# A feed-forward first product by seven block products instead of eight, in two of three channel-tile pairs

## The chip, the core and the metric

The kernel runs on one core of a Trainium2 chip. The metric is the device time of one execution in microseconds (us). The engines that matter here are PE (TensorE, the matrix products), DVE (VectorE) and ACT (ScalarE), which prepare its operands, POOL (GpSimd), and SP, whose queue starts the loads from device memory.

## What is computed

One layer of a streaming encoder over 256 tokens and 2048 channels: a mixer of three branches (a gated linear recurrence, an attention with forget gates, a multi-scale pooling), an output projection, and then the part that changes here, a gated feed-forward network (FFN) with 5632 inner channels.

```python
    x = x + merged @ w_out
    h2 = rms_norm(x, g_ffn)
    gate, up = jnp.split(h2 @ w_ffn_in, 2, axis=-1)
    return x + (jax.nn.silu(gate) * up) @ w_ffn_out
```

`h2 @ w_ffn_in` is called the first product here and the product with `w_ffn_out` the second. A final norm follows.

## The kernel before

All operands are float32, and every product is taken in three parts: each number is split into a high part and a low part (`float32r`), and high times high, high times low and low times high are added up. A weight block arrives by a load of 1 MB on SP's queue (`load`, line 59, three buffers), and `split` (line 64) makes the two parts of 1024 columns at a time: ACT copies to `whi` (line 69), DVE subtracts to get `wlo` (line 70). Four pairs of `whi` and `wlo` exist (pool `hl`, line 46), so the splits can stand at most four half blocks ahead of PE.

The activations lie transposed, channels on the partitions. `mm_t` (line 79) takes for each contraction tile of 128 a product of 512 columns, `whi` against both parts of the activations, and one of 256 columns, `wlo` against the high part; this pair of instructions does three parts. `evac_t` (line 95) adds the two halves. `mm_n` (line 87) does the same as three products of 256 columns into one place, and is used for the last tile of the second product alone.

Up to the FFN the order is: the mixer, `mT` (the merged branches, as two parts), the output projection (line 571, 16 tiles), which also writes `h2` (the FFN's input times its norm gain, in the tile called `hT`). The FFN's first product (line 590) runs over 44 channel tiles; each takes two column blocks with K = 2048 (`proj_t`, one for the gate and one for the up half), 32 pairs of products in all, and its result goes to `act` in two parts. The second product (line 613) runs over 16 output tiles, each with 44 contraction tiles. A scheduler sets the order on each engine; splits and evacuations may overtake other work (`tc.high_priority`). Each engine works through its instructions in that order, and SP's queue its loads; a wait at the front holds everything behind it.

Of the kernel before, what the change touches and what calls it, by code (L numbers as in the profile page):

```python
# [7 lines left out]
F32 = mybir.dt.float32  # L8
# [30 lines left out]
def block_kernel(ctx: ExitStack, tc: tile.TileContext, xT, vec,  # L39
# [5 lines left out]
    raw_p = ctx.enter_context(tc.tile_pool(name="raw", bufs=3))  # L45
    hl_p = ctx.enter_context(tc.tile_pool(name="hl", bufs=4))
    acc_p = ctx.enter_context(tc.tile_pool(name="acc", bufs=4, space=bass.MemoryType.PSUM))
    aux_p = ctx.enter_context(tc.tile_pool(name="aux", bufs=4, space=bass.MemoryType.PSUM))
    hT_p = ctx.enter_context(tc.tile_pool(name="hT", bufs=1))
    sm = ctx.enter_context(tc.tile_pool(name="sm", bufs=2))  # L50

# [34 lines left out]
    # the same in columns 0..255 alone: a longer product, a shorter way out  # L86
# [8 lines left out]
    def evac_t(ps, dst, scale=1.0):  # L95
        """Adds the two halves of a transposed product, times scale, into dst [128, 256]."""
# [17 lines left out]
    hT = hT_p.tile([P, KD, 2 * T], F32R, name="hT")  # [hi | lo] of x * g_mix, transposed  # L114
    vecs = const.tile([P, NV], F32, name="vecs")
    x_p = ctx.enter_context(tc.tile_pool(name="x", bufs=1))
    xt = x_p.tile([P, KD, T], F32, name="xt")  # x, then the residual stream, transposed
# [4 lines left out]
    vhl = at_p.tile([P, 2, 2, DB], F32R, name="vhl", bufs=1)  # token tile, part, channel  # L122
# [5 lines left out]
    warm = aux()  # keeps the array clocked up until the first operands are there  # L128
# [3 lines left out]
    def prepare_x(k):  # L132
        """Contraction tile k of x * g_mix as two parts, and its share of the sum of squares."""
# [12 lines left out]
    def rsqrt_mean(dst, ss, n, pool, nm):  # L146
        """dst (or two factors of it) = (ss / D + eps) ** -0.5, with one Newton step behind the table's root."""
# [45 lines left out]
    for c in (0, 2):  # keep where query >= key  # L193
# [3 lines left out]
    tri = at_p.tile([P, 2, T], F32, name="tri", bufs=1)  # 1 where row s (+128) <= t  # L197
# [4 lines left out]
    # F(query) - F(key) as one product: LF holds F^T and minus the selector of a head, RF the  # L202
    # selector and F^T; F in rows 0.. (high part) and 32.. (low), or 64.. and 96..
# [12 lines left out]
    def stats():  # L216
        """The factors 1 / rms(x), along the rows and in columns."""
# [10 lines left out]
    def normalise(k):  # L228
        """Contraction tile k of h, in the place of that of x * g_mix."""
# [43 lines left out]
    # minus half of log a for a recurrence gate of one  # L273
# [29 lines left out]
    def scores(h, q, k):  # L303
        """Softmax of head h's scores, transposed: [keys 0 | queries 0, 1], [keys 1 | queries 1]."""
# [10 lines left out]
        ns = at_p.tile([P, 3 * P], F32, name="ns")  # minus the scores  # L315
        st = at_p.tile([P, 8], F32, name="st")  # minus the maxima, sums, their reciprocals
# [77 lines left out]
    def lru_in(g):  # L394
# [22 lines left out]
        # gelu(y) = y (1 + tanh(c (y + 0.044715 y^3))) / 2  # L417
# [8 lines left out]
    def lru_out(g, u, uh, ul, ga):  # L426
# [14 lines left out]
        # th = tanh(-log(a) / 2): 1 - a = 2 th / (1 + th), 1 - a^2 = (1 - a)(1 + a).  # L441
# [7 lines left out]
        V.scalar_tensor_tensor(rg, rg, 2.0, rc, ALU.mult, ALU.mult)  # 1 - a  # L449
# [18 lines left out]
    def pool_in(g):  # L468
# [6 lines left out]
        # sums over 2, 4, 8, 16 tokens, each from the one before; column c holds token c - PADW  # L475
# [6 lines left out]
        # the mean, less the token itself: the first tokens count what there is  # L482
# [29 lines left out]
    def gate(n):  # L512
        """Sigmoid of gate block n = 3 m + branch."""
# [21 lines left out]
    mx_p.release()  # L535
    mT_p = tc.alloc_tile_pool(name="mT", bufs=1)
# [23 lines left out]
    h2 = hT_p.tile([P, KD, 2 * T], F32R, name="hT")  # [hi | lo] of x2 * g_ffn, transposed  # L560
# [8 lines left out]

    s2acc = const.tile([P, T], F32, name="sacc")  # L570
    for m in range(KD):
# [3 lines left out]
        g_ = vecs[:, GF + m:GF + m + 1]  # L575
        with tc.high_priority(offset=AHEAD):
            V.tensor_add(xt[:, m, :], xt[:, m, :], o)
            S.activation(h2[:, m, :T], xt[:, m, :], AF.Copy, scale=g_)
            V.scalar_tensor_tensor(h2[:, m, T:], xt[:, m, :], g_, h2[:, m, :T].bitcast(F32),  # L579
                                   ALU.mult, ALU.subtract)  # L580
        squares(m, s2acc)
    mT_p.release()
    sg_p.release()
    yAC_p.release()
    yB_p.release()

# [1 line left out]
    ac_p = tc.alloc_tile_pool(name="act", bufs=1)  # L588
    act = ac_p.tile([P, NF, 2 * T], F32R, name="act")
    for f in range(NF):  # L590
        pg = proj_t(wffi[2 * f], lambda k: h2[:, k, :])
        pu = proj_t(wffi[2 * f + 1], lambda k: h2[:, k, :])
        if f == 0:
            ps = aux()
            PE.matmul(ps[:, :T], lhsT=ones, rhs=s2acc, start=True, stop=True)
            R2 = const.tile([P, T], F32, name="R2")
            rsqrt_mean(R2, [ps[:, :T]], T, sm, ("t0", "t1"))
        gt = sm.tile([P, T], F32, name="t0")
        up = sm.tile([P, T], F32, name="t1")
        evac_t(pg, gt)  # L600
        V.tensor_mul(gt, gt, R2)
        S.activation(gt, gt, AF.Silu)
        evac_t(pu, up)
        G.tensor_mul(up, up, R2)  # L604
        V.tensor_mul(gt, gt, up)
        S.copy(act[:, f, :T], gt)
        V.tensor_sub(act[:, f, T:], gt, act[:, f, :T].bitcast(F32))

# [4 lines left out]
    for m in range(KD):  # L613
        ps = acc()
        for a in range(0, NF, 16):
            n = min(16, NF - a)
            r = load(wffo[m, :, a * P:(a + n) * P], n * P)
            for c in range(0, n, 8):
                nk = min(8, n - c)
                hi, lo = split(r, c * P, nk * P)  # L620
                k0 = a + c
                if m == last and k0 == 32:  # the sums over all blocks but this
                    pss = [aux()[:, :1] for _ in range(2)]
# [3 lines left out]
                (mm_n if m == last else mm_t)(ps, hi, lo, lambda k, k0=k0: act[:, k0 + k, :], nk,  # L627
                                              k0 == 0, k0 + nk == NF)
        g_ = vecs[:, GL + m:GL + m + 1]
        if m < last:  # L630
            o = sm.tile([P, T], F32, name="t0")
            evac_t(ps, o)
# [93 lines left out]
```

## Time and profile before

| | us |
|---|---|
| median of three runs | 1574.26 (1574.19 to 1574.32) |
| span of the profiled execution | 1572.5 |
| FFN's first and second product, first matmul to the last tile of the second product | 725.0 |
| PE busy in the span | 1549.3 |
| DVE busy in the span | 994.3 |
| ACT busy in the span | 821.3 |

The span runs from the first to the last instruction of the profiled execution; it is 1.8 us less than the median of the timed runs. Busy time of PE counts the pipelined tail of each matmul, so the distance between the starts of two matmuls, not the length of one, says what a matmul costs. The same holds in a small way on DVE and ACT, whose instructions overlap by about 0.09 us.

### The profile page before, as it was taken

The page shows a single profiled execution, that of the slowest core. Times are in us where ns is not written, and L with a number is a line of the kernel's source. Part 1 is how long each engine was busy: PE and PEld are TensorE (multiplying, and loading weights), DVE is VectorE, ACT ScalarE, POOL GpSimd, SP SyncE. Part 2 cuts the span into 40 slices and gives each one's busy share as a digit, 9 for nine tenths or more (in the row PEclk, how much of TensorE's full clock was granted, in tenths as well). Part 3 has the DMA queues.
Part 4 walks back from the last instruction along what each step waited for, and adds up shares of the span by engine and source line. Part 5 has one row for each costly group of instructions (what it writes and reads, how often), then busy time and mean ns, then how long its engine had stood idle before and what let it go on. Part 6 is the DMA issues. An engine that isn't in the chain of part 4 may idle for free.

```text
span 1572.5 us, 22842 instructions
## 1 busy us (share of the span) xinstructions
PE 1549.3 (99%) x8948; PEld 1362.1 (87%) x8948; DVE 994.3 (63%) x1356; ACT 821.3 (52%) x1264; POOL 154.8 (10%) x210
## 2 busy tenths in 40 slices
PE   8999999999999999999999999999999999999997
PEld 8888888888888888888888888888888888888886
DVE  9776677787565656667776555555555555445453
ACT  6565566666444444445555444444444444444442
POOL 7400011102000000000110000000000000010100
PEclk9999999999999999999999999999999999999998
DMA  7444455545555455555555555555555555555552
GB/s 245 170 155 159 140 184 185 212 164 200 185 190 197 167 202 184 201 174 201 188 188 183 189 189 189 188 188 188 188 188 187 188 188 178 188 196 178 192 187 88
DMA packets 46764, 288.92 MB, mean 184 GB/s; under 512 B 5184, under 2 KB 8000, under 8 KB 15936
## 3 DMA queue, kind: packets, MB, share of 16 engines
q1 hardware_dynamic: 46080, 286.54, 52.5%
q8 instruction: 70, 1.15, 0.3%
q10 hardware_dynamic: 576, 0.92, 0.2%
q14 instruction: 38, 0.31, 0.1%
HBM read 285.34 MB, written 2.10 MB: 183 GB/s over the span
## 4 chain that ended last, share of the span: by engine, by line
PE 93%; DVE 2%; POOL 2%; issue 2%; ACT 1%; DMA 0%; SPq 0%; DVEq 0%; POOLq 0%; ACTq 0%
PE acc L82 59%; PE acc L83 30%; POOL xn L232 1%; POOL part L144 1%; DVE wlo L70 1%; ACT whi L69 0%; POOL lev L479 0%; PE acc L91 0%; PE acc L93 0%; PE acc L92 0%; DVE xt L657 0%; PE aux L338 0%; DVE lma L179 0%; PE acc L264 0%; DMA raw<-in_wvf 0%
## 5 line engine op out<-in xcount | busy, mean ns | idle before, releaser
L82 PE MATMUL acc<-hT,whi 128*128 128x512 f32 x2800 | 983.6, 395 | 0.4 <-DVE hT L579 0.4
L70 DVE TENSOR_TENSOR wlo<-raw,whi 128x1024 fp32r<-128x1024 f32 (+2 forms) x554 | 671.3, 1213 | 476.5 <-ACT whi L69 475.5
L69 ACT CAST whi<-raw 128x1024 fp32r<-128x1024 f32 (+2 forms) x554 | 567.9, 1026 | 614.2 <-PE acc L82 425.1
L83 PE MATMUL acc<-hT,wlo 128*128 128x256 f32 x2800 | 785.6, 281 | 0.0
L82 PEld LDWEIGHTS acc<-hT,whi 128*128 128x128 f32 x2800 | 526.3, 188 | 122.2 <-DVE hT L579 0.7
L83 PEld LDWEIGHTS acc<-hT,wlo 128*128 128x128 f32 x2800 | 527.2, 188 | 0.2
L82 PE MATMUL acc<-act,whi 128*128 128x512 f32 x660 | 231.1, 395 | 0.0
L83 PE MATMUL acc<-act,wlo 128*128 128x256 f32 x660 | 185.1, 280 | 0.0
L82 PEld LDWEIGHTS acc<-act,whi 128*128 128x128 f32 x660 | 124.1, 188 | 29.1
L83 PEld LDWEIGHTS acc<-act,wlo 128*128 128x128 f32 x660 | 124.3, 188 | 0.0
L100 ACT COPY evt<-acc 128x256 f32<-128x256 f32 x247 | 90.0, 365 | 0.0
L82 PE MATMUL acc<-mT,whi 128*128 128x512 f32 x256 | 89.8, 395 | 0.0
L604 POOL TENSOR_TENSOR t<-t,R 128x256 f32<-128x256 f32 x44 | 32.4, 737 | 459.3 <-DVE t L101 435.0
L83 PE MATMUL acc<-mT,wlo 128*128 128x256 f32 x256 | 71.6, 280 | 0.0
L101 DVE TENSOR_TENSOR t<-acc,evt 128x256 f32<-128x256 f32 x167 | 69.7, 417 | 1.0 <-ACT evt L100 0.9
L568 POOL TENSOR_TENSOR sacc<-sacc,t 128x256 f32<-128x256 f32 x29 | 34.6, 1195 | 293.0 <-ACT t L567 293.0
L82 PEld LDWEIGHTS acc<-mT,whi 128*128 128x128 f32 x256 | 48.1, 188 | 11.4 <-DVE mT L554 0.3
L83 PEld LDWEIGHTS acc<-mT,wlo 128*128 128x128 f32 x256 | 48.2, 188 | 0.0
L551 POOL TENSOR_TENSOR t<-t,t 128x256 f32<-128x256 f32 x16 | 11.8, 740 | 352.3 <-DVE t L549 352.3
L82 PE MATMUL acc<-yB,whi 128*128 128x512 f32 x128 | 45.5, 395 | 0.0
L82 PE MATMUL acc<-yC,whi 128*128 128x512 f32 x128 | 45.5, 395 | 0.0
L82 PE MATMUL acc<-yA,whi 128*128 128x512 f32 x128 | 45.5, 395 | 0.0
(246 smaller groups left out, 1209.9 us busy)
## 6 DMA issues: line engine op xcount, KB each, us to landing
raw<-in_wffi SPq DMA_DIRECT2D x88, 1024.0 KB, 4.8
raw<-in_wgate SPq DMA_DIRECT2D x48, 1024.0 KB, 4.8
raw<-in_wffo SPq DMA_DIRECT2D x32, 1024.0 KB, 4.9
raw<-in_wqk SPq DMA_DIRECT2D x16, 1024.0 KB, 4.8
raw<-in_wxy SPq DMA_DIRECT2D x16, 1024.0 KB, 4.9
raw<-in_wbr SPq DMA_DIRECT2D x16, 1024.0 KB, 5.0
raw<-in_wout SPq DMA_DIRECT2D x16, 1024.0 KB, 4.8
raw<-in_wffo SPq DMA_DIRECT2D x16, 768.0 KB, 4.3
```

The source lines that it names most:

```text
L69: S.copy(hi[:, :n], r[:, a:a + n])
L70: V.tensor_sub(lo[:, :n], r[:, a:a + n], hi[:, :n].bitcast(F32))
L82: PE.matmul(ps, lhsT=hi[:, w], rhs=rhs(k), start=first and k == 0, stop=False)
L83: PE.matmul(ps[:, :T], lhsT=lo[:, w], rhs=rhs(k)[:, :T], start=False, stop=last and k == nk - 1)
L100: S.copy(tmp, ps[:, T:])
L101: V.tensor_add(dst, ps[:, :T], tmp)
L144: G.tensor_add(part, part, sq)
L232: G.tensor_mul(xn, xt[:, k, :], Rrow)
L551: (G if b == 1 else V).tensor_add(tot, tot, o)
L568: G.tensor_add(sacc, sacc, sq)
L604: G.tensor_mul(up, up, R2)
```

## The change

The FFN's first product works on groups of two channel tiles: 22 groups, in four chunks of 6, 6, 6 and 4, and after each chunk the second product is taken over that chunk's channels and added to the residual stream `xt`. Operands change sides: the activations (`hs`, 128 tokens at a time) are the stationary operand and the weights the moving one, and results come out with tokens on the partitions.

A group is a 2 x 2 block product: tokens (two halves) and K (two halves) against K and the gate and up columns (256 each). `group_plain` takes the eight block products. `group_strassen` takes seven (Winograd's form of Strassen's scheme), for which the weights are needed as sums of blocks and the activations as well; the activations' four sums are made once, in the output projection (`forms`). `PATTERN` makes groups 0, 1, 3, 4, ... of the seven kind (15) and 2, 5, ... of the eight kind (7). Each block product is 24 matmuls of 256 columns. Of the four sums of weight blocks in a seven-product group, `y` and the first `x` are made by DVE (`ADDS[0]`, `ADDS[1]`), and two more are added onto `x` by DMAs that POOL issues (`accum_op`), between the splits of `x`.

The results are transposed back on PE (`turn`, four transposes a group) into `act`, which now holds one chunk. The second product uses `mm_n` everywhere. For the FFN the raw buffers become six of 8 KB (`raw6`), which are allocated on the side where `mT` and the three old raw buffers lay.

```diff
+PATTERN = (1, 1, 0)
+ADDS = ("v", "v", "dma", "dma")
+CHUNKS = (12, 12, 12, 8)
...
+    mT_p = tc.alloc_tile_pool(name="mT", bufs=1, side="right")
...
+    hs = hs_p.tile([P, KB, 8, 2, P], F32R, name="hs")
...
+    def forms(k, first, src):
+        n = src.shape[1]
+        S.copy(hs[:, k, first:first + n, 0, :], src)
+        V.tensor_sub(hs[:, k, first:first + n, 1, :], src, hs[:, k, first:first + n, 0, :].bitcast(F32))
...
+            hm = hg[:, k, :] if m < KB else hg_p.tile([P, T], F32, name="hm", bufs=2)
+            S.activation(hm, xt[:, m, :], AF.Copy, scale=vecs[:, GF + m:GF + m + 1])
+            hm = hm.rearrange("p (a b) -> p a b", a=2)
+            forms(k, m // KB * 2, hm)
+            if m >= KB:
+                a11, a21, a12, a22 = hg[:, k, :P], hg[:, k, P:], hm[:, 0, :], hm[:, 1, :]
+                c = hg_p.tile([P, 4, P], F32, name="hc", bufs=2)
+                V.tensor_sub(c[:, 1, :], a11, a21)
+                V.tensor_add(c[:, 2, :], c[:, 1, :], a22)
+                V.tensor_sub(c[:, 3, :], a12, c[:, 2, :])
+                V.tensor_sub(c[:, 0, :], a21, a22)
+                forms(k, 4, c)
         squares(m, s2acc)
+    hg_p.release()
     mT_p.release()
...
-    for f in range(NF):
-        pg = proj_t(wffi[2 * f], lambda k: h2[:, k, :])
-        pu = proj_t(wffi[2 * f + 1], lambda k: h2[:, k, :])
...
+    raw_p.release()
+    raw_p = tc.alloc_tile_pool(name="raw6", bufs=6, side="right", reuse_waits="tile")
...
+    def parts(r):
+        got = []
+        for h in range(2):
+            w = r[:, :, h * 512:(h + 1) * 512]
+            hi = hl_p.tile([P, 2, 512], F32R, name="whi")
+            lo = hl_p.tile([P, 2, 512], F32R, name="wlo")
+            with tc.high_priority(offset=AHEAD):
+                S.copy(hi, w)
+                V.tensor_sub(lo, w, hi.bitcast(F32))
+            got.append((hi, lo))
+        return got
+
+    def product(ps, ws, forms_, start, stop, more=False):
+        for h, (hi, lo) in enumerate(ws):
+            for o, f in zip(ps, forms_):
+                for part, w in ((0, hi), (1, hi), (0, lo)):
+                    for j in range(4):
+                        k = 4 * h + j
+                        PE.matmul(o, lhsT=hs[:, k, f, part, :], rhs=w[:, :, j * P:(j + 1) * P],
...
+    def blocks(i):
+        src = wffi[4 * i:4 * i + 4].rearrange("(j s) p (h c) -> s h p j c", s=2, h=2)
+        got = {}
+        for s, h in ((1, 0), (1, 1), (0, 0), (0, 1)):
+            got[s, h] = raw()
+            nc.sync.dma_start(got[s, h], src[s, h])
+        return got[0, 0], got[0, 1], got[1, 0], got[1, 1]
+
+    def add(dst, a, b, how):
+        with tc.high_priority(offset=AHEAD):
+            if how == "dma":
+                G.dma_start(dst, b, accum_op=ALU.add)
+            else:
+                V.tensor_add(dst, a, b)
...
+    def group_strassen(i):
+        b11, b21, x, b22 = blocks(i)
+        y = raw()
+        add(y, b11, x, ADDS[0])
+        add(x, x, b22, ADDS[1])
+        A, B, C = bank(), bank(), bank()
+        product([C], parts(x), [5], True, True, True)
+        add(x, x, b11, ADDS[2])
+        product([B], parts(y), [4], True, True, True)
+        n5 = tmp("n5")
+        S.copy(n5, B)
+        product([A], parts(b11), [0], True, True, True)
+        m1 = tmp("m1")
+        S.copy(m1, A)
+        product([B], parts(x), [6], False, True, True)
+        add(x, x, b21, ADDS[3])
+        s = tmp("s")
+        V.tensor_sub(s, B, m1)
+        d = tmp("d")
+        V.tensor_sub(d, n5, s)
+        V.tensor_sub(s, s, C)
+        product([A], parts(b21), [2], False, True, True)
+        g0 = tmp("g0")
+        S.activation(g0, A, AF.Silu, scale=r2[:, 0:1])
+        product([B], parts(b22), [7], False, True, True)
+        V.tensor_sub(m1, B, m1)
+        product([C], parts(x), [3], False, True, True)
+        V.tensor_add(d, d, C)
+        S.activation(d, d, AF.Silu, scale=r2[:, 1:2])
+        return gated(0, m1, m1, g0), gated(1, s, s, d)
+
+    def group_plain(i):
+        b11, b21, b12, b22 = blocks(i)
+        c = [[bank(), bank()] for _ in range(2)]
+        product([c[0][0], c[1][0]], parts(b11), [0, 1], True, False)
+        product([c[0][0], c[1][0]], parts(b21), [2, 3], False, True)
...
+    def turn(a, f):
+        tp = aux_p.tile([P, 2, T], F32, name="turn")
+        for j in range(2):
+            for t in range(2):
+                PE.transpose(tp[:, j, t * P:(t + 1) * P], a[t][:, j * P:(j + 1) * P],
+                             ident.bitcast(F32))
+        S.copy(act[:, f:f + 2, :T], tp)
+        V.tensor_sub(act[:, f:f + 2, T:], tp, act[:, f:f + 2, :T].bitcast(F32))
...
+    for ci, n in enumerate(CHUNKS):
+        final = ci == len(CHUNKS) - 1
+        late = None
+        for f in range(0, n, 2):
+            got = (group_strassen if PATTERN[done % len(PATTERN)] else group_plain)(done)
+            done += 1
+            if late is not None:
+                turn(*late)
+            late = got, f
+        for m in range(KD):
+            ps = acc_p.tile([P, T], F32, name="bank")
+            r = raw_p.tile([P, 2048], F32, name="raw")
+            nc.sync.dma_start(r[:, :n * P], wffo[m, :, f0 * P:(f0 + n) * P])
...
+                mm_n(ps, hi, lo, lambda k, c=c: act[:, c + k, :], nk, c == 0, c + nk == n)
+            V.tensor_add(xt[:, m, :], xt[:, m, :], ps)
```

Two places show the order. The first is SP's queue where the loads of the output projection (`in_wout`) end and those of the first product (`in_wffi`) begin. Before:

```order
L61 DMA raw_7921<-in_wout 128x2048 [waits DMAHW6_49,DVE_49]
L61 DMA raw_7974<-in_wout 128x2048 [waits DMAHW7_49,DVE_49]
L61 DMA raw_8035<-in_wffi 128x2048 [waits DMAHW0_49,DVE_49]
L61 DMA raw_8078<-in_wffi 128x2048 [waits DMAHW1_49,DVE_49]
L61 DMA raw_8148<-in_wffi 128x2048 [waits DMAHW2_49,DVE_49]
```

After, at the same place (`raw_8156`, `raw_8158`, `raw_8160`, `raw_8162` are x, b22, b11 and b21 of group 0):

```order
L63 DMA raw_7994<-in_wout 128x2048 [waits DMAHW6_49,DVE_49]
L63 DMA raw_8056<-in_wout 128x2048 [waits DMAHW7_49,DVE_49]
L663 DMA raw_8156<-in_wffi 128x2x1024 [waits PE_49,Pool_49]
L663 DMA raw_8158<-in_wffi 128x2x1024 [waits DMAHW2_49,DVE_49]
L663 DMA raw_8160<-in_wffi 128x2x1024 [waits DMAHW0_49]
L663 DMA raw_8162<-in_wffi 128x2x1024 [waits DMAHW1_49]
```

The first load of the first product waited for a split of DVE; now it waits for PE, because its buffer lies where `mT` was, and the other three stand behind it in the queue.

The second place is DVE inside the first product. Before, in two channel tiles in a row:

```order
L70 TENSOR_TENSOR wlo_9494<-raw_9491,whi_9493 128x1024
L70 TENSOR_TENSOR wlo_9498<-raw_9491,whi_9497 128x1024
L101 TENSOR_TENSOR t1_9434<-acc_9390,evt_9440 128x256
L605 TENSOR_TENSOR t0_9433<-t0_9433,t1_9434 128x256
L70 TENSOR_TENSOR wlo_9551<-raw_9548,whi_9550 128x1024
L607 TENSOR_TENSOR act_8033<-t0_9433,act_8033 128x256
L70 TENSOR_TENSOR wlo_9555<-raw_9548,whi_9554 128x1024
L101 TENSOR_TENSOR t0_9533<-acc_9447,evt_9535 128x256
```

After, in the middle of group 6, a seven-product group with another behind it (`raw_10478` is its x, `raw_10484` b21, `raw_10480` b22; `raw_10742` is y of group 7):

```order
L642 TENSOR_TENSOR wlo_10564<-raw_10482,whi_10563 128x1024
L642 TENSOR_TENSOR wlo_10594<-raw_10478,whi_10593 128x1024
L642 TENSOR_TENSOR wlo_10598<-raw_10478,whi_10597 128x1024
L642 TENSOR_TENSOR wlo_10632<-raw_10484,whi_10631 128x1024
L642 TENSOR_TENSOR wlo_10636<-raw_10484,whi_10635 128x1024
L642 TENSOR_TENSOR wlo_10666<-raw_10480,whi_10665 128x1024
L699 TENSOR_TENSOR s_10626<-bank_10490,m1_10591 128x256
L642 TENSOR_TENSOR wlo_10670<-raw_10480,whi_10669 128x1024
L701 TENSOR_TENSOR d_10628<-n5_10557,s_10626 128x256
L672 TENSOR_TENSOR raw_10742<-raw_10738,raw_10734 128x2048
L642 TENSOR_TENSOR wlo_10699<-raw_10478,whi_10698 128x1024
L642 TENSOR_TENSOR wlo_10703<-raw_10478,whi_10702 128x1024
```

The splits of x stand in DVE's order at the places where the added sums are wanted, and the next group's sum y of 2048 columns stands ahead of the last split of x.

## Rows read from the trace of the kernel before

**Rows 1.** The page: span, busy time and share of each engine, and the chain's engines.

```profile
span 1572.5 us, 22842 instructions
PE 1549.3 (99%) x8948; PEld 1362.1 (87%) x8948; DVE 994.3 (63%) x1356; ACT 821.3 (52%) x1264; POOL 154.8 (10%) x210
...
PE 93%; DVE 2%; POOL 2%; issue 2%; ACT 1%; DMA 0%; SPq 0%; DVEq 0%; POOLq 0%; ACTq 0%
```

**Rows 2.** Timeline of PE: start, length, line; idle before it in brackets.

```profile
818.41 0.39 PE L82 MATMUL acc<-hT,whi 128*128 128x512 f32 x1
...
824.58 0.50 PE L82 MATMUL acc<-hT,whi 128*128 128x512 f32 x1 [0.41 <-DVE hT L579]
...
830.29 0.59 PE L595 MATMUL aux<-sacc,ones 128*128 128x256 f32 x2
830.54 0.58 PE L82 MATMUL acc<-hT,whi 128*128 128x512 f32 x1
830.96 0.28 PE L83 MATMUL acc<-hT,wlo 128*128 128x256 f32 x1
...
1543.44 0.28 PE L91 MATMUL acc<-act,whi 128*128 128x256 f32 x1
...
1554.34 0.28 PE L91 MATMUL acc<-act,whi 128*128 128x256 f32 x1
```

**Rows 3.** Timeline of all engines at a head's transposes: start, length, engine, line.

```profile
120.97 0.37 PE L338 MATMUL aux<-ident,ph 128*128 128x128 f32 x3
...
121.18 0.42 PE L338 MATMUL aux<-ident,pl 128*128 128x128 f32 x3
...
121.44 0.46 PE L82 MATMUL acc<-hT,whi 128*128 128x512 f32 x1
```

**Rows 4.** Stretches, output projection and first product: length, busy us of each engine, clock, DMA.

```profile
734.00:818.40 84.40, 84.40 (x482) 73.65 (x482) 60.52 (x76) 46.28 (x75) 13.80 (x14) 1.00 0.54 188
818.40:1343.44 525.04, 524.63 (x2998) 458.60 (x2997) 313.03 (x420) 257.26 (x374) 33.66 (x46) 1.00 0.53 186
```

**Rows 5.** Timeline of DVE in the first and the second product.

```profile
999.96 1.23 DVE L70 TENSOR_TENSOR wlo<-raw,whi 128x1024 fp32r<-128x1024 f32 x1 [1.58 <-ACT whi L69]
1001.10 0.42 DVE L101 TENSOR_TENSOR t<-acc,evt 128x256 f32<-128x256 f32 x1
1002.44 0.42 DVE L605 TENSOR_TENSOR t<-t,t 128x256 f32<-128x256 f32 x1 [0.92 <-POOL t L604]
1002.78 1.22 DVE L70 TENSOR_TENSOR wlo<-raw,whi 128x1024 fp32r<-128x1024 f32 x1
...
1006.70 0.42 DVE L101 TENSOR_TENSOR t<-acc,evt 128x256 f32<-128x256 f32 x1
1007.15 0.42 DVE L601 TENSOR_TENSOR t<-t,R 128x256 f32<-128x256 f32 x1
...
1457.34 0.69 DVE L70 TENSOR_TENSOR wlo<-raw,whi 128x512 fp32r<-128x512 f32 x1 [1.15 <-ACT whi L69]
```

**Rows 6.** Groups by line and shape: count, busy us, mean ns, idle before.

```profile
L69 ACT CAST whi<-raw 128x1024 fp32r<-128x1024 f32 x512 | 535.8, 1047 | 587.1 <-PE acc L82 412.1 <-issue 170.2 <-PE acc L92 1.5
L568 POOL TENSOR_TENSOR sacc<-sacc,t 128x256 f32<-128x256 f32 x29 | 34.6, 1195 | 293.0 <-ACT t L567 293.0
L604 POOL TENSOR_TENSOR t<-t,R 128x256 f32<-128x256 f32 x44 | 32.4, 737 | 459.3 <-DVE t L101 435.0 <-DVE R L161 13.8 <-PE acc L82 10.5
```

**Rows 7.** The page's DMA parts: SP's queue, and the median landing of a load.

```profile
q1 hardware_dynamic: 46080, 286.54, 52.5%
...
raw<-in_wffi SPq DMA_DIRECT2D x88, 1024.0 KB, 4.8
```

**Rows 8.** Stretches at the very end; columns as in rows 4.

```profile
1559.40:1560.40 1.00, 0.15 (x2) 0.00 (x0) 0.42 (x1) 0.30 (x1) 0.00 (x0) 1.00 0.00 0
...
1563.40:1564.40 1.00, 0.26 (x2) 0.00 (x0) 0.71 (x3) 0.00 (x0) 0.00 (x0) 0.50 0.00 0
```

More of the change, by code (lines that the diff above doesn't have):

```diff
@@ L111, in proj_t @@
         return ps
-    hT = hT_p.tile([P, KD, 2 * T], F32R, name="hT")
     vecs = const.tile([P, NV], F32, name="vecs")
@@ L117, in block_kernel @@
     xt = x_p.tile([P, KD, T], F32, name="xt")
+    hT_p = tc.alloc_tile_pool(name="hT", bufs=1)
+    hT = hT_p.tile([P, KD, 2 * T], F32R, name="hT")
     yB_p = tc.alloc_tile_pool(name="yB", bufs=1)
@@ L557, in block_kernel @@
                 gate(len(sigs))
-    h2 = hT_p.tile([P, KD, 2 * T], F32R, name="hT")
+    sg_p.release()
+    yAC_p.release()
+    yB_p.release()
+    hT_p.release()
+    hs_p = tc.alloc_tile_pool(name="hs", bufs=1)
+    hs = hs_p.tile([P, KB, 8, 2, P], F32R, name="hs")
+    hg_p = tc.alloc_tile_pool(name="hg", bufs=1)
+    hg = hg_p.tile([P, KB, T], F32, name="hg")
     def squares(m, sacc):
@@ new lines, in raw @@
+    def raw():
+        return raw_p.tile([P, 2, 1024], F32, name="raw")
+    def parts(r):
[16 more added lines that the diff above has]
+                        PE.matmul(o, lhsT=hs[:, k, f, part, :], rhs=w[:, :, j * P:(j + 1) * P],
+                                  start=start and h == 0 and part == 0 and w is hi and j == 0,
+                                  stop=stop and h == 1 and w is lo and j == 3, skip_group_check=more)
@@ new lines, in tmp, with gated @@
+    def tmp(nm):
+        return ft_p.tile([P, T], F32, name=nm)
+    def gated(t, a, up, g):
+        V.scalar_tensor_tensor(a, up, r2[:, t:t + 1], g, ALU.mult, ALU.mult)
+        return a
+    def group_strassen(i):
[28 more added lines that the diff above has]
+        return gated(0, m1, m1, g0), gated(1, s, s, d)
@@ new lines, in group_plain @@
+    def group_plain(i):
[3 more added lines that the diff above has]
+        product([c[0][0], c[1][0]], parts(b21), [2, 3], False, True)
+        g = [tmp("g0"), tmp("d")]
+        for t in range(2):
+            S.activation(g[t], c[t][0], AF.Silu, scale=r2[:, t:t + 1])
+        product([c[0][1], c[1][1]], parts(b12), [0, 1], True, False)
+        product([c[0][1], c[1][1]], parts(b22), [2, 3], False, True)
+        return [gated(t, tmp(("m1", "s")[t]), c[t][1], g[t]) for t in range(2)]
@@ new lines, in turn @@
+    def turn(a, f):
+        tp = aux_p.tile([P, 2, T], F32, name="turn")
+        for j in range(2):
+            for t in range(2):
+                PE.transpose(tp[:, j, t * P:(t + 1) * P], a[t][:, j * P:(j + 1) * P],
+                             ident.bitcast(F32))
+        S.copy(act[:, f:f + 2, :T], tp)
+        V.tensor_sub(act[:, f:f + 2, T:], tp, act[:, f:f + 2, :T].bitcast(F32))
+    pss = [aux_p.tile([P, 2, T], F32, name="turn")[:, 0, :1] for _ in range(2)]
+    for t in range(2):
+        PE.matmul(pss[t], lhsT=s2acc[:, t * P:(t + 1) * P], rhs=ones[:, :1], start=True, stop=True)
@@ L610, in block_kernel @@
+    r2a, r2b = rsqrt_mean(None, pss, 2, const, ("r2ms", "r2rt"))
+    r2 = const.tile([P, 2], F32, name="r2")
+    V.tensor_mul(r2, r2a, r2b)
     s3acc = const.tile([P, T], F32, name="sacc")
@@ L612, in block_kernel @@
     last = KD - 1
[L613 to L619, printed above, removed]
-                hi, lo = split(r, c * P, nk * P)
-                k0 = a + c
-                if m == last and k0 == 32:
-                    pss = [aux()[:, :1] for _ in range(2)]
+    f0 = done = 0
+    for ci, n in enumerate(CHUNKS):
[11 more added lines that the diff above has]
+            nc.sync.dma_start(r[:, :n * P], wffo[m, :, f0 * P:(f0 + n) * P])
+            for c in range(0, n, n // 2):
+                nk = n // 2
+                hi, lo = split(r, c * P, nk * P)
+                if late is not None and c:
+                    turn(*late)
+                    late = None
+                if final and m == last and c:
+                    pss = [aux_p.tile([P, 2, T], F32, name="turn")[:, 0, :1] for _ in range(2)]
                     for t in range(2):
@@ L649, in block_kernel @@
     diag = sm.tile([P, T], F32, name="t0")
-    R3 = aux()
+    R3 = aux_p.tile([P, 2 * T], F32, name="turn")
     for t in range(2):
@@ L660, in block_kernel @@
             (nc.sync if m % 4 else S).dma_start(out[:, first:m + 1, :], xt[:, first:m + 1, :])
-    ac_p.release()
+    raw_p.release()
+    ft_p.release()
+    act_p.release()
+    hs_p.release()
+    aux_p.release()
+    acc_p.release()
 def _blocks(w, k):
```

69 lines of the change are left out of this document (24 added, 45 removed).

## The prediction

> **What bounds the kernel now.** I read the page's engine shares and its chain first: PE is busy for 1549.3 of 1572.5 us and is 93% of the chain that ended last [rows 1]. So the question is what a matmul costs and what could make PE wait. Next the timeline of PE, where starts count and not lengths. From the first matmul of the FFN (818.41) to the first of its last tile (1543.44) stand 1408 + 660 = 2068 pairs of 512 and 256 columns. Without one wait of 0.41 and one extra product that takes 0.43 (830.29 to 830.96 less one product of 512 columns, 0.24) that is 724.2 us, or 0.350 a pair [rows 2]. The last tile takes triples of 256 columns: 31 in 1543.44 to 1554.34, 0.352 a triple, 0.117 a product [rows 2]. Per column the two forms cost the same. PE stood still for 0.41 us in the first product; DVE was busy for 313 of its 525 us, ACT for 257, the DMA engines for 53% [rows 4]. There is no other bound near in the mean; the change gives more work to DVE and the DMA engines, so each group has to be looked at by itself.
>
> **PE's work.** Before, a group (two channel tiles) is 64 pairs, 22.4 us. After, seven products of 24 matmuls are 168 x 0.117 = 19.7 us, eight are 22.5. In all 15 x 168 + 7 x 192 = 3864 matmuls, 452.9 us, against 1408 x 0.350 = 493.1: **-40.2**. The second product turns 660 pairs into triples: **+0.9**. The 88 transposes are new. Nearest are the attention's, six in 0.47 us (120.97 to 121.44), 0.078 each [rows 3]: **+6.9**. These are of plain float32; the extra product at 830.29, plain float32 of 256 columns, took 0.43, so 128 columns would take 0.21 and the 88 together 19. I take the first, a transpose like them, and keep 12 us more for the range.
>
> **The start of the first product.** Before, its loads came while the output projection ran. After, the first load (x) waits for PE's last read of `mT`, and b22, b11 and b21 stand behind it on SP's queue. A load lands after 4.8 us [rows 7]; the queue's 286.54 MB took 52.5% of the span, 2.88 us for a MB, so each of the next two lands 3.0 later. DVE's order has y = b11 + x first and so needs the third load: 10.8 us. Then come two sums of 2048 columns on DVE. A split of 1024 columns takes 1.23, one of 512 takes 0.69, so 2048 take 2.3, and 2.2 from start to start, as 1.14 for 1024 (999.96 to 1001.10) [rows 5]. Then ACT's copy of half a block, 1.05 [rows 6]. 10.8 + 2 x 2.2 + 1.05 = 16.3 us in which PE has nothing, less the 0.4 of before: **+15.9**. The FFN norm's factors and the last `forms` lie beside this. In the output projection DVE was busy for 60.5 of 84.4 us, 4.0 of 5.6 a tile [rows 4]; `forms` adds at most 1.3 us to a tile in eight of sixteen, so the splits cover it: 0, and 8 x 1.3 = 10 us if that cover were gone.
>
> **DVE in a seven-product group.** 14 splits x 1.14 = 16.0; two sums, 4.4; seven small operations of 256 columns at 0.34 to 0.45 (1002.44 to 1002.78; 1006.70 to 1007.15) [rows 5], 2.8; the transposes' second part, 0.6: **23.8 us against PE's 19.7**. ACT's 14 copies at 0.96 (1.05 less the overlap) and five small ones stay under 17. In an eight-product group DVE has 8 x 1.14 and three small ones, 11 us, against 22.5. So DVE is behind in two groups of three, and can make up only what the four split buffers and the order let it: two products' splits (4.6 us) and the next group's sums (4.4), 9.0 us.
>
> **The accumulating DMAs.** A new operation, with no row. Each starts when x has been split, and the next split of x waits for its landing at the front of DVE's queue; everything behind it waits as well. What covers it is what DVE's order has in between: for the first, the splits of y and b11, 4.6 us; for the second, the splits of b21 and b22, two small operations and, where a seven-product group follows, its y, 7.6 us (6.3 where an eight-product group follows). Its time A I bound from below by a load of the same size, 4.8 [rows 7]. From above: it has to read two operands for each result, so 2.9 us more of the DMA engines, and can stand beside a load in flight, as much again: 10.6. POOL's own part in issuing it has no row either; its nearest instructions, sums of 256 columns, take 0.74 to 1.20 us [rows 6], which the upper end allows for in place of part of a meeting. I take 7.7, one more read than a load. The waits are then 3.1 and 0.1 in the first group of a pair, 3.1 and 1.4 in the second. SP's next load of b11 waits for the first DMA as well, and lands 4.8 us later; y, its first user, is 7.6 us of DVE work away, so that is hidden.
>
> On this price the Trainium skill, Collectives: The Full Stack, section "The bandwidth ceiling: the fold count and why AG ≠ RS ≠ AR", speaks against the change: an addition in the DMA engines needs two source reads, and a reduction there moved 32.35 GB/s where a copy moved 62.28. By the load row alone the sum below would be +16, by the Trainium skill's ratio (4.8 and once more 2.9 x 0.93, 7.5) about what it is with 7.7. No run here shows it yet.
>
> **The sum.** A pair of seven-product groups takes DVE 2 x 23.8 + 7.7 = 55.3; 9.0 are done during the eight-product group ahead; the last product follows, 2.8: 49.1 us, where PE alone needs 39.4 and 0.6 for transposes. That is 9.1 a pair, **+64** for seven. DVE doesn't get its 9.0 everywhere: within a pair the next group's y (2.2) stands ahead of the last split of x, and DVE, held to PE's pace by four buffers, comes to it late: **+15.4** for seven pairs. The first pair has no eight-product group ahead: **+4.6**. The last, single one: 23.8 + 4.5 - 9.0 + 2.8 - 19.7 = **+2.4**. Together -40.2 + 0.9 + 6.9 + 15.9 + 64 + 15.4 + 4.6 + 2.4 = +70. On the span of 1572.5, with 1.8 us between it and the median of the runs, that is **1644 us**. With A = 4.8 the same sum is +16 (1590), with A = 10.6 it is +157 (1731).
>
> **The rivals.**
> 1. Faster: the DMAs land within the 4.6 us of two splits, and DVE gets far enough ahead in the eight-product groups that its 4 us more in each of the others never reach PE. For it: DVE's total in three groups is 59 us, PE's 62. Against it: only four split buffers, and a plain load's row is already 4.8. Then -40.2 + 0.9 + 6.9 + 15.9 = -16.5: 1558. It decides at A = 4.6; above it each us costs up to two for a seven-product group.
> 2. Much slower: the DMA engines are the bound. In a seven-product group they move four loads (12 us) and two additions with two reads each (12), 24 us of a group of 27, so additions and loads stand in each other's way: A at 10 or more, 1715 to 1760.
> 3. Slower by little: A between 4.6 and 5.5, as a load, 1580 to 1605.
> 4. The clock. At the end the granted clock was still 1.00 in 1559.4 to 1560.4 and 0.50 in 1563.4 to 1564.4, after some 4 us with little on PE [rows 8]. The wait at the start is longer. A product of 24 matmuls at the lower level takes 2.8 us more; where DVE is late this is hidden, so some 3 to 10 us, inside the range.
>
> **How the numbers follow.** The forecast (A 5.5 to 9.5, 1605 to 1700): 0.5. Rival 2: 0.22. Rival 3: 0.12. Faster: 0.12. Within 0.2% (3 us, about what a measurement of this kernel can tell from no change): 0.04, where rival 1 loses part of its gain. So faster 0.12, same 0.04, slower 0.84. The range 1577 to 1742 leaves out rival 1 and the same case (0.15) and the top of rival 2 (0.05); the bound of A above, 1731, is in it.
>
> **What would show it.** In the profile after: a wait of PE of about 16 us ahead of the first product, whose first load was issued when the output projection had ended; matmuls of 256 columns 0.117 apart; transposes 0.08 apart; the additions' time to landing, 7.7; waits of DVE's splits (or ACT's copies) for a DMA, twice a group; seven-product groups of 24 to 25 us and eight-product groups of 22.5. It is wrong if PE's pitch differs, if the additions land within 4.6 us, or if DVE's sums of 2048 columns are not near 2.2.

## The result, and the profile after

| | before | after |
|---|---|---|
| median of the runs | 1574.22 us | 1661.0 us |
| ratio, with its 95% interval | | 1.0548 (1.0533 to 1.0563) |
| span of the profiled execution | 1572.5 us | 1658.3 us |

The change makes the kernel 5.5% slower. The forecast was 1644 us, in a range from 1577 to 1742. The spans differ by 86 us, and the forecast's sum had 70.

First the page of after: the span and the engines (beside [rows 1]), the groups of the first product's matmuls and splits, the queues and the DMA issues (beside [rows 7]).

```profile
span 1658.3 us, 26770 instructions
PE 1556.8 (94%) x10746; PEld 1453.5 (88%) x10746; DVE 1165.7 (70%) x1503; ACT 899.5 (54%) x1315; POOL 139.0 (8%) x196
...
q1 hardware_dynamic: 59648, 286.54, 50.4%
q0 software_dynamic: 4320, 31.46, 10.0%
...
L653 PE MATMUL bank<-whi,hs 128*128 128x256 f32 x2576 | 378.1, 291 | 72.1 <-DVE s L702 45.0
L642 DVE TENSOR_TENSOR wlo<-raw,whi 128x1024 fp32r<-128x1024 f32 x266 | 317.9, 1222 | 117.3 <-ACT whi L641 111.7
L670 POOL DMA_DIRECT2D raw<-raw x30 | 25.9, 864 | 737.4 <-DVE wlo L642 641.5
L672 DVE TENSOR_TENSOR raw<-raw 128x2048 f32<-128x2048 f32 x30 | 68.6, 2287 | 9.0 <-DMA raw<-in_wffi 5.3
raw<-in_wffi SPq DMA_DIRECT2D x88, 1024.0 KB, 5.2
raw<-raw POOLq DMA_DIRECT2D x30, 1024.0 KB, 7.8
```

PE is busy for about as many us as before, but its share of the span fell from 99% to 94%: it waits now, and by what ended the waits mostly for DVE's line 702. The sums of 2048 columns take DVE 2.29 us, the accumulating DMAs 7.8 from issue to landing.

Next PE's timeline at the start of the first product, as in [rows 2].

```profile
818.36 0.28 PE L85 MATMUL acc<-mT,wlo 128*128 128x256 f32 x1
821.87 0.61 PE L737 MATMUL turn<-ones,sacc 128*128 128x1 f32 x4 [3.23 <-POOL sacc L581]
835.41 2.08 PE L653 MATMUL bank<-whi,hs 128*128 128x256 f32 x8 [12.93 <-ACT whi L641]
```

The first product starts at 835.41 where it started at 818.41. Eight matmuls take 2.08 us here; at the full clock eight take 1.1. The third view is the four stretches of the first product (six groups, six, six and four): length, PE's busy time, the mean granted clock, the DMA engines' share and GB/s, and the sum.

```profile
835.41:989.62 154.21, 139.28 (x1077) 0.93 0.76 220
1057.80:1208.71 150.91, 135.03 (x1079) 0.94 0.76 225
1276.91:1427.84 150.93, 133.96 (x1079) 0.95 0.77 225
1496.02:1597.53 101.51, 89.90 (x711) 0.93 0.73 205
sum 557.56, PE 498.18; mean PE 124.54
```

Before, the same product was 1408 pairs by 0.350, 492.8 us without its wait of 0.41, at a clock of 1.00 [rows 2, 4]. Now it takes 557.6, 64.8 more, and PE stands still for 59.4 of it. The start is 17.0 us later, less that wait 16.6. Together that is 81 of the 86 us.

Where does PE wait? A list of waits from 836 to 1600 us (engine, line, what it waited for: us, times, longest) and the chain of work that ended last, in a seven-product group (start, us, what):

```profile
DVE wlo L642 <- ACT whi L641: 111.7, 95, 5.7
ACT whi L641 <- DMA raw<-raw: 79.0, 22, 6.1
PE bank L653 <- DVE s L702: 45.0, 11, 6.6
PE bank L653 <- ACT n L692: 7.6, 7, 2.1
```

```profile
1494.84 8.50 DMA raw<-raw
...
1503.44 1.06 ACT whi L641
...
1507.18 6.98 DMA raw<-raw
...
1514.26 1.05 ACT whi L641
...
1516.48 1.22 DVE wlo L642
1517.70 2.20 DVE raw L672
1519.90 0.34 DVE s L702
...
1520.38 13.48 PE bank L653 x92
```

The chain goes from one accumulating DMA through ACT's copy and DVE's split of x to the next, twice a group, then through a sum of the next group (line 672) and the subtraction of line 702 to PE. Line 702 reads the bank of the first product, and the last product of the group is added up in that bank: PE may not start it earlier. By the timelines of PE and DVE, 34 of the 45 us of these waits are in the first group of a pair, where a sum of the next group stands ahead of line 702; in the other groups it stands right behind a late split of x.

Last the clock, in stretches of 2 us after that wait: length, PE's busy time, granted clock, DMA share, GB/s.

```profile
1514.00:1516.00 2.00, 0.59 (x6) 1.00 0.41 53
...
1518.00:1520.00 2.00, 0.00 (x0) 0.71 0.73 213
1520.00:1522.00 2.00, 1.62 (x7) 0.50 0.97 397
1522.00:1524.00 2.00, 2.00 (x11) 0.50 0.06 20
1524.00:1526.00 2.00, 2.00 (x12) 0.58 0.65 131
1526.00:1528.00 2.00, 2.00 (x19) 1.00 0.97 197
```

PE stood still from 1514.6 to 1520.4; the clock went to 0.50 (1.2 GHz) towards the end of that and stayed there for five more us of matmuls. The view counts 11 of them in 2 us where it counts 19 at 1.00 (a matmul that reaches over an edge is counted on both sides of it).

### The profile page after: what moved, and what is told of

Its sections match the earlier page's. It is cut to its first block, busy times and chain, and to the rows that moved or that the text cites. A ratio compares the mean times of both kernels' runs of the same rounds, so it can differ in the third digit from the quotient of the medians.

```text
span 1658.3 us, 26770 instructions
## 1 busy us (share of the span) xinstructions
PE 1556.8 (94%) x10746; PEld 1453.5 (88%) x10746; DVE 1165.7 (70%) x1503; ACT 899.5 (54%) x1315; POOL 139.0 (8%) x196
## 3 DMA queue, kind: packets, MB, share of 16 engines
q0 software_dynamic: 4320, 31.46, 10.0%
## 5 line engine op out<-in xcount | busy, mean ns | idle before, releaser
L72 DVE TENSOR_TENSOR wlo<-raw,whi 128x1024 fp32r<-128x1024 f32 (+4 forms) x410 | 460.8, 1125 | 276.5 <-ACT whi L71 273.3
L71 ACT CAST whi<-raw 128x1024 fp32r<-128x1024 f32 (+4 forms) x410 | 388.9, 950 | 373.0 <-PE acc L84 196.2
L84 PE MATMUL acc<-hT,whi 128*128 128x512 f32 x1392 | 490.1, 395 | 0.0
L653 PE MATMUL bank<-whi,hs 128*128 128x256 f32 x2576 | 378.1, 291 | 72.1 <-DVE s L702 45.0
L653 PEld LDWEIGHTS bank<-whi,hs 128*128 128x128 f32 x2576 | 345.3, 198 | 77.2 <-issue 31.6
L642 DVE TENSOR_TENSOR wlo<-raw,whi 128x1024 fp32r<-128x1024 f32 x266 | 317.9, 1222 | 117.3 <-ACT whi L641 111.7
L641 ACT CAST whi<-raw 128x1024 fp32r<-128x1024 f32 x266 | 270.9, 1047 | 232.6 <-PE bank L653 102.2
L85 PE MATMUL acc<-hT,wlo 128*128 128x256 f32 x1392 | 390.7, 281 | 0.0
L85 PEld LDWEIGHTS acc<-hT,wlo 128*128 128x128 f32 x1392 | 262.0, 188 | 0.2
L93 PE MATMUL bank<-act,whi 128*128 128x256 f32 x704 | 197.3, 281 | 0.0
L94 PE MATMUL bank<-act,whi 128*128 128x256 f32 x704 | 197.3, 280 | 0.0
```

The source lines that it names most:

```text
L84: PE.matmul(ps, lhsT=hi[:, w], rhs=rhs(k), start=first and k == 0, stop=False)
L85: PE.matmul(ps[:, :T], lhsT=lo[:, w], rhs=rhs(k)[:, :T], start=False, stop=last and k == nk - 1)
L93: PE.matmul(o, lhsT=hi[:, w], rhs=rhs(k)[:, :T], start=first and k == 0, stop=False)
L94: PE.matmul(o, lhsT=hi[:, w], rhs=rhs(k)[:, T:], start=False, stop=False)
L641: S.copy(hi, w)
L642: V.tensor_sub(lo, w, hi.bitcast(F32))
```

## The experiments

All ratios are to the kernel before, which ran beside each.

**The two DMAs taken out, with their sums.**

```diff
-ADDS = ("v", "v", "dma", "dma")
+ADDS = ("v", "v", "none", "none")
```

(`add` does nothing for "none".)

> The two accumulating DMAs of every seven-product group are left out, and with them two of its four sums: the products take x as it stands, so this part of the computation is missing. All matmuls, splits and loads are as after. Theory (the DMAs' time to landing is what DVE and PE wait for): by the prediction's sum with no DMA in it, -40.2 + 0.9 + 9.7 (transposes at the measured 0.11) + 15.9 + 10 (DVE's 23.8 a group still beside 19.7) + 15.4 (order) = +12: about 1588, between 1570 and 1610. Rival (DVE's own work, PE's clock after each wait and the order of the sums hold the time, the DMAs lie beside them): above 1635. What the first rival or the theory leave of PE's waits ahead of the last product (45 us after) shows the order's share: the theory keeps about 2 us a group.

Measured: 1607.8 us, ratio 1.0214 (1.0197 to 1.0231), at the upper end of the theory's range; the rival is out. The two DMAs and the waits for them cost 53 us. PE's waits and the four stretches' sum, as above:

```profile
PE bank L653 <- DVE s L704: 24.4, 7, 3.7
```

```profile
sum 505.27, PE 480.91; mean PE 120.23
```

What is left of the waits, 24.4 us, is one for each pair of seven-product groups, and ends with the same subtraction (line 704 here). On DVE it stands behind two sums of the next group, y and x + b22:

```profile
1056.96 2.28 DVE L674 TENSOR_TENSOR raw<-raw 128x2048 f32<-128x2048 f32 x1
...
1060.30 2.28 DVE L674 TENSOR_TENSOR raw<-raw 128x2048 f32<-128x2048 f32 x1
1062.50 0.41 DVE L704 TENSOR_TENSOR s<-s,bank 128x256 f32<-128x256 f32 x1
```

**All four sums on DVE.** `ADDS = ("v", "v", "v", "v")`.

> All four sums of a seven-product group on DVE, no accumulating DMA. DVE has 28.2 us a group in place of 23.8, and no wait for a landing. Theory (waits for the DMAs cost what the sum says): pairs 2 x 28.2 - 9.0 + 2.8 - 40.0 = 10.2, seven of them +71, start +15.9, order +15.4, transposes +9.7, products -39.3, the first and the last group +7: +80, 1654, so near the 1661 of after (1635 to 1670). Rival (DVE is the bound anyway and the DMAs are free beside it): 30 x 2.2 = 66 more than after, 1727.

Measured: 1668.1 us, ratio 1.0594 (1.0579 to 1.0610): inside the theory's range, the rival's 1727 is out. In the mean a DMA that DVE waits for saves next to nothing against a sum of 2.3 us that DVE makes itself: 7 us for 30 of them. PE's waits are 65.2 us in 15 groups, and they are for another line than after: line 699, which reads the bank that the product with b22 needs. DVE's timeline in one such group (the first line is the sum x + b21), and PE's:

```profile
1098.27 2.29 DVE L672 TENSOR_TENSOR raw<-raw 128x2048 f32<-128x2048 f32 x1
1100.47 5.76 DVE L642 TENSOR_TENSOR wlo<-raw,whi 128x1024 fp32r<-128x1024 f32 x5
...
1106.48 0.41 DVE L699 TENSOR_TENSOR s<-bank,m 128x256 f32<-128x256 f32 x1
```

```profile
1107.04 2.05 PE L653 MATMUL bank<-whi,hs 128*128 128x256 f32 x8 [3.84 <-DVE s L699]
```

The reader of that bank stands behind the sum and five splits.

**Only one of the two by DMA.** `ADDS = ("v", "v", "dma", "v")` and `("v", "v", "v", "dma")`.

> Of the two late sums the first (x + b11) stays an accumulating DMA, the second is DVE's. Theory (a DMA costs its 7.8 less the DVE work between the split of x and its next split; for the first that is 4.6): 26.0 us of DVE work a group and 3.1 of waiting, 2 x 29.1 - 9.0 + 2.8 - 40.0 = 12.0 a pair, where four sums on DVE have 10.2: 1668 + 7 x 2 = 1682 (1672 to 1692). Rival (only the number of DMAs counts, through the DMA engines or a fixed cost of each): the same as with the second alone, 1655 to 1668.

> Of the two late sums the second (x + b21) stays an accumulating DMA, the first is DVE's. Theory: its cover is 7.6 or 6.3 us of DVE work, so it waits 0.1 and 1.4: 2 x 26.0 + 1.5 - 9.0 + 2.8 - 40.0 = 7.3 a pair, 33 less in all than with the first alone, and 20 less than four sums on DVE: 1640 to 1655. Rival (only the number counts): as with the first alone, 1655 to 1668.

Measured: 1694.8 us, ratio 1.0766 (1.0750 to 1.0782), with the first alone, and 1657.1, ratio 1.0527 (1.0509 to 1.0544), with the second alone. Each is 2 to 3 us above the theory's range, and 1657.1 alone would fit the rival as well; but the two differ by 37.7 us for the same 15 DMAs of the same size (landing after 8.1 and 8.2 us), where the theory gave 33 and the rival nothing. PE's waits of the first and of the second kernel:

```profile
PE bank L653 <- DVE s L699: 65.9, 15, 6.2
```

```profile
PE bank L653 <- DVE s L702: 50.5, 12, 7.3
```

So the number of DMAs alone doesn't set the time. That it is the cover (what DVE can do between the issue and the next split of the same buffer) is not shown by this pair: with the second sum on DVE, making the first by DMA costs 27 us (1668.1 to 1694.8) where the theory gave 13 (12.0 and 10.2 a pair), and with the second by DMA it costs 4 (1657.1 to 1661.0) where the theory gave 13 as well (9.1 and 7.3 a pair). The first of the two kernels also has its waits for line 699, as with all sums on DVE, and the second for line 702. DVE's order around the second sum is thus a rival for the 37.7, and no run separates the two.

**Each add in two halves.**

```diff
-                G.dma_start(dst, b, accum_op=ALU.add)
+                for h in (slice(0, 512), slice(512, 1024)):
+                    G.dma_start(dst[:, :, h], b[:, :, h], accum_op=ALU.add)
```

> Each accumulating DMA is cut in two, one for each half of the contraction, so that ACT's copy and DVE's split of the first half need only the first. Theory (PE's waits are the time to landing less its cover, and the transfer is part of that time): the first half lands 1.5 to 3 us sooner, which the two adds of a group give back where they are late; 1625 to 1650. Rival (the time to landing is mostly a fixed part, and POOL issues twice as often at 0.86): 1655 or above.

Measured: 1633.4 us, ratio 1.0392 (1.0357 to 1.0426), as the theory had it. Its reason is only half right. By the page of this kernel's profile the halves land no sooner after their issue than the whole:

```profile
raw<-raw POOLq DMA_DIRECT2D x60, 512.0 KB, 7.7
```

So what the halves give is that the first one can be issued when half of x has been split, and that its half can be split again while the second is under way (issues at 1058.12 and 1060.63, copies of the halves at 1067.30 and 1069.80). Which of the two gives more wasn't taken apart.

**The late sums on POOL**, in two halves, no DMA.

> The two late sums of a seven-product group are made by POOL, in two halves of 1024 columns, no accumulating DMA. POOL's sums of 256 columns took 0.74 to 1.20, so a half is 2.4 to 4.8 and a sum 5 to 9.6 us, as long as a DMA in all, but its first half is there early and the DMA engines move nothing for it. Theory (what costs is when x is ready): near the kernel without the two sums, 1608, up to 1630 with 4.8 a half. Rival (POOL and DVE hinder each other, so that DVE's splits take longer, or the sums come as late as the DMAs): 1640 or above.

Measured: 1681.0 us, ratio 1.0678 (1.0662 to 1.0694): the rival's. POOL's half sums took 3.14 us, within the forecast; but DVE's splits became slower, 1641 ns in the mean against 1222 after. Their minimum, median and maximum (ns), and the two groups of the page:

```profile
L642 DVE TENSOR_TENSOR wlo<-raw,whi x266: 1205/1212/3434, 834.8 to 1616.1; 128x1024 fp32r<-128x1024 f32 x133
```

```profile
L642 DVE TENSOR_TENSOR wlo<-raw,whi 128x1024 fp32r<-128x1024 f32 x266 | 428.5, 1641 | 39.4 <-ACT whi L641 38.7
...
L676 POOL TENSOR_TENSOR raw<-raw 128x1024 f32<-128x1024 f32 x60 | 187.8, 3139 | 601.2 <-DVE wlo L642 586.9
```

At least half of the splits are as fast as ever, some last 3.4 us, 2.2 longer: 266 x 0.42 = 111 us more of DVE's time in the splits, beside 60 sums of POOL. The Trainium skill, SBUF — State Buffer, section "Who interferes with whom", says that a DVE instruction with two SBUF inputs contends with a GpSimd instruction that reads SBUF; the trace agrees, by 3.43 us for a split that takes 1.21 otherwise.

**Eight products in every group**: `PATTERN = (0,)`.

> Every group by eight products; what is left of the change is the new operand layout, the load order at the start, products of 256 columns, the transposes and the second product's triples. No sums at all. Theory: products +1.8 in both halves, transposes +9.7, the start +11 to +13 (the first product takes b11, the third load: 10.8 and one copy and split): +24, 1598 (1592 to 1606). Rival (the new form has waits of its own, by its banks, its clock or its loads, that the prediction put down to the sums): above 1615.

Measured: 1606.7 us, ratio 1.0206 (1.0191 to 1.0221), 0.7 above the theory's range. PE has no wait in the first product but the first (start 829.67, 7.59 of waiting): the four stretches are busy throughout.

```profile
sum 510.20, PE 510.20; mean PE 127.55
```

A group with its four transposes takes 23.2 us: the transposes of line 730 come at 900.53 and again at 923.74.

```profile
900.53 0.27 PE L730 MATMUL turn<-ident,m 128*128 128x128 f32 x1
900.64 0.27 PE L730 MATMUL turn<-ident,s 128*128 128x128 f32 x1
...
923.74 0.27 PE L730 MATMUL turn<-ident,m 128*128 128x128 f32 x1
```

Less four by 0.11 that is 22.76, 0.1185 a matmul; before, it was 64 by 0.350, 22.4. So 32 us of the change's 87 are there without a single product less: 10.9 at the start, 22 x 0.8 = 17.6 in the groups, and 2.2 by the lower clock of the first five us (the first stretch took 140.8, the second, of as many groups, 138.6); the last us no row names.

**A bank of its own for the last product.**

```diff
-        product([C], parts(x), [3], False, True, True)
-        V.tensor_add(d, d, C)
+        E = bank()
+        product([E], parts(x), [3], True, True, True)
+        V.tensor_add(d, d, E)
```

With the DMAs in place (the first product's bank is then no longer added into d; this sum is missing):

> The last product of a seven-product group goes into a bank of its own, so PE need not wait until DVE has subtracted the first product's bank (line 702), which stands behind a sum of the next group on DVE. Theory A (the split of x behind the DMA ends last, the bank only seems to): 1655 to 1666, as after. Theory B (the bank's reader ends last, some 4 us after the first half of the split, and PE's lower clock after the longer idle comes on top): 15 groups by 2.5 to 5 us less, 1590 to 1625.

and with the two late sums left out as well:

> The two late sums are left out and the last product has a bank of its own (the first product's bank is not added to its result), so both parts of the computation are missing. Theory (without the DMAs what is left, 24.4 us of waits and some 12 to 15 of low clock, comes from the sum x + b22 of the next group that stands ahead of the reader of the bank, line 702 after): PE goes on without it: 1570 to 1585. Rival (DVE's 23.8 a group beside 19.9 of PE: the wait only moves to the splits, as it did with the DMAs in): 1598 to 1608.

Measured: 1654.4 us, ratio 1.0508 (1.0493 to 1.0524), and 1586.9, ratio 1.0079 (1.0064 to 1.0094). With the DMAs in, the bank is worth 7 us, close to theory A: the waits for line 702 are gone, and others stand in their place. PE's waits in that kernel:

```profile
PE bank L653 <- ACT whi L641: 38.7, 25, 2.9
```

Without them it is worth 21 (1607.8 to 1586.9), which leaves 2 us above the theory's range. The waits fall from 24.4 to 9.8 and none is over 1.6 us; the stretches' sum and the second of them:

```profile
PE bank L653 <- ACT whi L641: 9.8, 7, 1.6
```

```profile
1038.99:1170.46 131.47, 128.56 (x1078) 1.00 0.56 195
...
sum 484.26, PE 474.05; mean PE 118.51
```

Here the clock is 1.00 from the second stretch on, so this kernel gives PE's own work: 3 x 128.6 + 84.4 (the last stretch's) = 470 us for the same matmuls that kept PE busy for 498.2 after. The difference, 28 us, is the lower clock. In the kernel without the two sums it is 481 - 470 = 11.

**The start.** Twice I tried to let the first loads go ahead. The first try gave x, b22 and b11 other buffers by changing the order in which these are named.

> In the first group x, b22 and b11 take the places of old raw buffers, and the sum y a free place beside act, so that the loads need not wait for PE's last read of mT; b21 alone does. Theory (the start's 16.4 us are three loads behind mT): they land during the output projection, and what is left is the norm's 3.2 us and a sum, a copy and a split, 2.2 + 1.05 + 1.2 in part hidden: a wait of 4 to 7 us, 1648 to 1653 in all. Rival (the first group is held by DVE's order and the sums anyway, so that the gain is given back there): the first product starts earlier but the first group ends as late, 1656 to 1661.

Measured: 1660.7 us, ratio 1.0549 (1.0533 to 1.0565), nothing. It says nothing of the theories: a place is given out at a buffer's first use, x kept the one over `mT`, and its load was again issued when PE was done, at 818.42. The second try uses up the first place:

```diff
+        if i == 0:
+            G.memset(raw()[:, 0, :1], 0.0)
+            order = ((1, 0), (0, 0), (1, 1), (0, 1))
```

> One byte column of the first place is written by POOL ahead of the first loads, so that x takes an old raw buffer, and b11, then b22 are loaded behind it: x and b11 need not wait for PE's last read of mT, b22 does. Theory (the start's wait is three loads in a row behind mT): only one load of 4.8 stands behind mT, so PE starts at 827 to 829 in place of 835.4 and the kernel takes 1650 to 1655. Rival (the first groups are held by DVE, and the time is given back by their end): PE starts earlier, but the second group ends where it did; 1657 to 1662.

Measured: 1656.0 us, ratio 1.0517 (1.0502 to 1.0533). The load of x is issued at 808.96 and the first product starts earlier:

```profile
829.51 2.08 PE L653 MATMUL bank<-whi,hs 128*128 128x256 f32 x8 [7.33 <-ACT whi L641]
```

That is 5.9 us earlier than after, and the second stretch of the first product begins at 1051.24, 6.6 earlier: what is won at the start is kept. The medians differ by 5.0, just outside the theory's range; the mechanism is shown, the last us of it isn't.

**Groups that alternate**, seven products and eight, with POOL's sums.

> Groups alternate (seven products, eight products), the two late sums on POOL in halves, the first loads early: 11 seven-product groups in place of 15. DVE has 23.8 + 11 = 35 us in a pair where PE has 42.6, so no seven-product group stands behind another one. Theory (the waits and the low clock come from two seven-product groups in a row): eight products throughout took 1606.7; 11 x 2.8 = 31 less, 5 to 9 less at the start: 1566 to 1572, at or a little below before. Rival (each seven-product group has a wait of its own, some 3.5 us and the clock): 1585 or above.

Measured: 1615.6 us, ratio 1.0262 (1.0246 to 1.0277), in the rival's range. But it doesn't decide between the two: POOL's sums slowed the splits here as well (1526 ns in the mean), PE's waits are 16 of 0.5 to 1.7 us for a split and 10 of 0.8 for line 712's tile, and only 0.8 us stand against line 706, which reads the first product's bank. The loads were arranged as in the first try at the start, with as little effect (the first product starts at 834.56). No version tried beats the kernel before.

## Why the prediction was right, and where not

**The verdict and the main step hold.** The prediction said that DVE, which makes seven-product groups in 23.8 us where PE needs 19.7, is late, and that each accumulating DMA adds what its 7.7 us are longer than DVE's work beside it. The sums took 2.29 and the DMAs 7.8; without the DMAs and their sums the kernel is 53 us shorter, where of the prediction's +70 about 60 hang on the wait for them (9 are left without it: -40.2 + 0.9 + 6.9 + 15.9 + 10 + 15.4); and of one DMA alone the first is the dear one, by 37.7 us where the covers of 4.6 and 7.6 gave 33. That the cover makes this difference is argued: DVE's order around the second sum changes with it.

**What was mis-sized.** Term by term, the first product:

| term | forecast | measured |
|---|---|---|
| PE's own work, with 18 x 4 transposes | -40.2 + 5.6 = -34.6 | 470 - 492.8 = -23 |
| PE's waits and the lower clock | 64 + 15.4 + 4.6 + 2.4 = 86.4 | 59.4 + 28 = 87 |
| the start | +15.9 | +16.6 |
| the rest (second product, its transposes, the end) | +0.9 + 1.3 = 2.2 | 86 - 81 = 5 |

- The step that failed is PE's work. I took 0.117 a matmul (452.9 us for 3864) from a row of the second product, and the first product's come at 0.1185 (groups of 23.2 us). For a transpose I took 0.078 from the attention's rows, but those transpose `float32r` tiles (`ph` and `pl`, line 338), and the new ones of plain float32 came 0.11 apart, between the two bounds. In 3864 matmuls and 72 transposes that is 5.0 + 2.3 = 7 of the 12 us; the other 5 no row names (waits too short to be listed would be such).
- The sum of waits came out right for a partly wrong reason. I counted no lower clock where DVE is late ("hidden") and 3 to 10 us in all. PE waited for 59.4 us and lost 28 more to the lower clock; only together are they the 87 that were forecast as DVE's lateness. That the slow matmuls give DVE time as a wait does would explain the sum, but no run shows it. Nor is the loss all hidden: where the bank of its own took away the long waits, the kernel lost slow matmuls with them (1607.8 to 1586.9, 21 us, of which 14.6 were waits and 6.9 PE's busy time).
- The order's term named the wrong sum. The next group's y does stand ahead of the last split of x, but in the time in which that split waits for the DMA; what holds PE in the first group of a pair is the sum x + b22 behind it, ahead of line 702, and the bank that line 702 reads. The size, 15.4, was near the 21 that the bank alone gives without the DMAs, in part by luck: there y and x + b22 both stand ahead of the bank's reader. With the DMAs the bank gives 7; the split comes late anyway.

**The rivals.** Rival 1 wanted landings within 4.6 us; they took 7.8. Rival 2 had the DMA engines as the bound: they were busy for 0.76 of the first product (0.54 without the DMAs), a load landed after 5.2 and not 4.8, but an addition not after 10. The price was near the one chosen: queue 0 took 0.100 x 1658.3 / 31.46 = 5.27 us of the DMA engines for a MB where a load took 2.92, 1.81 times as much. The Trainium skill, Collectives: The Full Stack, section "The bandwidth ceiling: the fold count and why AG ≠ RS ≠ AR", has 62.28 GB/s for a copy beside 32.35 for a reduction, 1.93 times; the trace comes near it with 1.81.

**What stays open**: how the 28 us of lower clock divide between what DVE's lateness would have cost anyway and what they add; how much of the 37.7 us between the two DMAs is the cover and how much DVE's order; and whether seven-product groups that stand alone would do without waits, since the kernel that was to show it had POOL in DVE's way.

## What to carry to other kernels

Before replacing products by sums of operands, look whether the engine that makes the sums and splits has time in that very group, not in the mean of several, and in what order it works: here DVE's instructions take 23.8 us (the forecast's count) beside 19.9 of PE. Fifteen groups with an eighth of their products taken away were no faster than full ones even with half of the sums missing (1607.8 and 1606.7). They were faster, by 20 us, only when the last product had a bank of its own as well (1586.9), so much of what was lost there was the order and not DVE's work. An operation moved to a DMA isn't gone: its consumer waits for the landing, so look at what stands between the issue and the next use, or cut it so that its consumer can begin on a part (1661.0 to 1633.4 here). And look at what stands ahead of the reader of a buffer that PE wants back, not only at what produces PE's operands.

## What the runs showed of the hardware

- An accumulating DMA between two places in SBUF: 1 MB lands 7.8 us after its issue, half a MB 7.7 (two of them under way); POOL is held for 0.86 us by issuing it. It takes 5.27 us of the DMA engines for a MB where a load takes 2.92.
- POOL's sums of two SBUF tiles and DVE's stand in each other's way: splits of 1.21 us last up to 3.43 while POOL sums.
- After 5.8 us without a matmul the granted clock was 0.50 (1.2 GHz), and it stayed there for 5 us of matmuls (at the end of the kernel before, [rows 8], it had fallen in the same way); in the kernel with waits of at most 1.6 us it was 1.00 from the second stretch on.
- Transposes of plain float32, 128 by 128, came 0.11 us apart; the attention's, of `float32r`, had come 0.078 apart [rows 3].
